# Value products held back until two groups of transposes are done, in a two-layer attention kernel

## The chip, the core and the metric

The kernel runs on one core of one Trainium2 chip. The metric is the device time of one execution in microseconds (us); lower is better. In the text PE is the matrix engine (TensorE), DVE is VectorE, ACT is ScalarE, POOL is GpSimd.

## What is computed

The reference is a trunk of two layers on 2048 rows of width 1024, in float32. Each layer projects the normalised input, runs attention, gates the result, projects it out and adds it to the input. Cut to the attention:

```
# layer 0: 8 heads of forgetting attention ("fox") and 4 of differential attention ("diff")
p  = softmax(where(causal, q @ k.T * scale + F[q] - F[k], -inf));  out = p @ v           # fox
p  = softmax(s1) - lam * softmax(s2);                              out = p @ v           # diff
# layer 1: 16 heads of dilated windows, branches merged by their softmax sums
sc = where(window_of_256_keys, q_blocks @ k_band.T * scale, -inf)
m, l = max(sc), sum(exp(sc - m));  o = (exp(sc - m) / l) @ v_band
```

## The kernel before

The projections, the attention of layer 0, its output projection, the projections of layer 1, its attention and its output projection follow one another. The change touches the two attentions, which share one scheduler (`run`) and one transposing helper (`flip`).

**Slots.** Layer 0's attention works on eight pairs `p`: `p` below 4 is a pair of fox heads, the others are one diff head with its two softmax maps. A unit is one block of 128 queries (block `i` has `i + 1` key tiles of 128). Its key tiles are cut into groups: four tiles of two heads for fox, eight tiles of one map for diff. Layer 1's units (`dilated`) are two query tiles of one branch, with one or two groups of up to eight blocks. One group is one slot of `run`, and a group has a weight (its fourth entry): 1 for fox and dilated, 2 for a diff group of more than four key tiles.

**What a slot does.** `grp[0]` is `turn`: it calls `flip`, which transposes up to eight 128x128 blocks of probabilities on PE. Each block goes as two halves of 64 rows, into two PSUM tiles `t_ps` (tag `t`, three buffers in all); then ACT or DVE, by a counter, copies each of the two tiles into a half of one SBUF tile `pt`. `emit` then issues the pieces that are due, mostly scores for a unit some slots later (`LEAD` is 7, `DLEAD` is 4). A score piece is 6 or 12 matmuls into two PSUM tiles `s_ps` (tag `s`, three buffers), and DVE reduces both tiles into SBUF (lines L840, L843 and L845, or L1276). `flush` last issues the value products (`grp[1]`, `av`) of the slot before, from its `pt` into an `o_ps` tile (tag `o`, two buffers). [...]

**On PE** a slot is thus a run of transposes (L709, called T below), a score piece (L834 or L1268, S) and the value products of the slot before (L923 or L1309, O). T and S use 64 rows of the array at a time (`64*128` in the profile's shapes), O uses 128 rows (`128*64` for fox and dilated, `128*128` for diff). A value product stands twice in the profile's counts and once in the program order.

**Order.** The engines run their queues in order. The order inside a queue is fixed when the program is built: a scheduler takes the instructions about as they are written, and moves some where it expects a wait. The finishing steps of a unit (`grp[2]`, row sums and the merge of branches) are queued by `flush` and run at the start of a later unit. In the diff part they use a tile `sq`.

Of the kernel before, what the change touches and what calls it, by code (L numbers as in the profile page):

```python
# [8 lines left out]
F32 = mybir.dt.float32  # L9
# [74 lines left out]
def trunk(ctx: ExitStack, tc: tile.TileContext, A, out):  # L84
# [6 lines left out]
    def dma(o, i):  # L91
        if o.dtype == F32R:
            o = o.bitcast(F32)
        if i.dtype == F32R:
            i = i.bitcast(F32)
        return queue[0].dma_start(o, i)  # L96
# [7 lines left out]
    def dap(t, off, ap):  # L104
        return bass.AP(tensor=t.tensor, offset=t.offset + off, ap=ap)

    def pool(es, name, bufs=1, space=None, side=None):
        kw = {"space": space} if space is not None else {}
        if side is not None:
            kw["side"] = side  # L110
        return es.enter_context(tc.tile_pool(name=name, bufs=bufs, reuse_waits="tile", **kw))
# [538 lines left out]
    def run(units, early):  # L650

        later, pend, slots, at, T = [], [], [], [], 0
        begins = []
        for n, (_, groups) in enumerate(units):
            begins.append(T)
            for grp in groups:  # L660
                slots.append((n, grp))
                at.append(T)
                T += grp[3]
        todo = [(begins[n] + when, f) for n, (pieces, _) in enumerate(units) for when, f in pieces]
        todo.sort(key=lambda x: x[0])

        def emit(until):
            while todo and todo[0][0] < until:
                todo.pop(0)[1]()

        def follow(n):
            for x in [x for x in later if x[0] <= n]:
                later.remove(x)
                x[1]()

        def flush():
            for n, grp in pend:
                grp[1]()
                later.extend((n + d, f) for d, f in grp[2])
            pend.clear()  # L680

        emit(0)
        for i, (n, grp) in enumerate(slots):
            if i == 0 or slots[i - 1][0] != n:
                follow(n)
            grp[0]()
            emit(at[i] + grp[3])
            flush()
            pend.append((n, grp))
        flush()  # L690
        for _ in early():
            n += 1
            follow(n)
        for _, f in sorted(later, key=lambda x: x[0]):
            f()
# [20 lines left out]
    def to_rows(ap, ps, x, n, rd, k, w):  # L716

        TE.transpose(ps[0:n, 0:128], x, ident)
        rh = ap.tile([128, 128], F32R, tag="rh", name="rh", bufs=1)
        rl = ap.tile([128, 128], F32R, tag="rl", name="rl", bufs=1)  # L720
        SC.copy(rh[0:n], ps[0:n, 0:128])
        V.tensor_tensor(rl[0:n], ps[0:n, 0:128], rh[0:n].bitcast(F32), OP.subtract)
        dma(dap(rd, 0, [[128, n], [1, 128]]), rh[0:n])
        dma(dap(rd, k * w, [[128, n], [1, 128]]), rl[0:n])
# [11 lines left out]
    def attention0():  # L736
# [5 lines left out]
        ap2 = pool(es, "at2")  # L742
# [199 lines left out]
        def finish(p, half):  # L942

            rd = row_d[2 * (p % 4) + half]

            def rows():
                lt = lts[p, half]
                x = x_bank("x_ps")
                if p < 4:
                    V.reciprocal(lt, lt)  # L950
                    to_rows(ap2, x, lt.rearrange("p h t -> p (h t)"), 16, rd, 2, 1024)
                else:

                    l1 = lt[:, 0, :]
                    V.scalar_tensor_tensor(l1, l1, 128.0 * EPS, l1, OP.mult, OP.mult)
                    to_rows(ap2, x, l1, 8, rd, 1, 1024)

            def chunk(n):
                c = HALVES[half][n]
                cs = slice(512 * c, 512 * c + 512)  # L960
                r = rw[n]
                x = x_bank("bc_ps")
                if p < 4:
                    dma(r[0:4], dap(rd, 512 * n, [[1024, 4], [1, 512]]))
                    og = gates[p]
                    TE.matmul(x, sels[0][0:64], r[0:64], start=True, stop=True)
                    V.tensor_tensor(og[:, cs], x, og[:, cs], OP.mult)
                else:
                    dma(r[0:2], dap(rd, 512 * n, [[1024, 2], [1, 512]]))
                    og = ogs[p]  # L970
                    sq = ap2.tile([128, 512], F32, tag="sq", name="sq", bufs=2)
                    SC.activation(sq, og[:, cs], AF.Square)
                    TE.matmul(x, ones, sq, start=True, stop=False)
                    TE.matmul(x, sels[1], r, start=False, stop=True)
                    SC.activation(sq, x, AF.Ln, scale=1.0 / 128)
                    SC.activation(sq, sq, AF.Exp, scale=-0.5)
                    (V if p == 7 else PO).tensor_tensor(sq, sq, gates[p][:, cs], OP.mult)
                    V.scalar_tensor_tensor(og[:, cs], og[:, cs], subl, sq, OP.mult, OP.mult)
                dma(og_d[0][c][p], og[:, cs])

            return [(1, rows), (LATE[p == 7][0], lambda: chunk(0)), (LATE[p == 7][1], lambda: chunk(1))]

        lts, Os, ogs, raws = {}, {}, {}, []
# [3 lines left out]
        def early():  # L987
# [10 lines left out]
            box.extend((wo, ps_p, (yield from first_rows(0, wo, ps_p, *ts, lambda e: split_raw(e) if e > 5 else None, 8))))  # L998

        run(units, early)  # L1000
        es.close()
        return box
# [1 line left out]

    WO_AT = [(0, 3), (0, 5), (0, 7), (1, 1), (1, 6), (1, 7)]
    LATE = ((3, 4), (2, 2))
    LEAD, PT_BUFS = 7, 3
    wo_es = ExitStack()
    wo_tiles = attention0()

# [135 lines left out]
    def dilated():  # L1146
# [252 lines left out]
        def early():  # L1399
# [6 lines left out]
            box.extend((wo, ps_p, (yield from first_rows(1, wo, ps_p, *ts, more_weights, 7))))  # L1406

        run([unit(p, c, br, half) for p in range(8) for c in range(4) for half in range(2) for br in range(2)], early)
        es.close()
        return box  # L1410
# [57 lines left out]
```

## Time and profile before

| | us |
|---|---|
| median of three runs | 3220.56 (3219.57 to 3225.43) |
| the profiled execution: its time | 3230.95 |
| the profiled execution: its span, first to last instruction | 3228.9 |
| PE busy in the span | 3080.9 (95%) |
| fox part, 798 to 1190 us | 392 |
| diff part, 1190 to 1562 us | 372 |
| dilated part, 2503 to 3013 us | 510 |

The profiled execution is 10.4 us longer than the median of the runs. Ends of matmuls are modelled, so distances between matmuls are read from their starts. "Busy" counts a matmul that is held up inside a run of matmuls as busy too; a wait of PE can therefore hide in a run that is longer than others of its kind.

### The profile page before, as it was taken

Reading aid. Unit: us, or ns where it says so; the run is one execution under the profiler, and the core shown is the slowest. Engines: PE = TensorE matmul, PEld = TensorE weight load, DVE = VectorE, ACT = ScalarE, POOL = GpSimd, SP = SyncE. Lnnn points to the kernel's source line nnn. Section 1 sums busy time; section 2 is a strip of 40 time slices with the busy share of each in tenths; the row PEclk is TensorE's granted clock in tenths of the full one; section 3 lists DMA queues with packets and bytes.
Section 4 is the critical chain, followed back from the end, with each engine's and each line's share of the span. In section 5 each row is a group of like instructions: output and inputs, shape, how many; then the busy total and the mean of one; then the engine's idle time right before and its main releaser. Section 6 shows DMA issues by size and latency. Waiting matters only on the chain. (4 is left out here: it accounts for less than half of the span.)

```text
span 3228.9 us, 60884 instructions
## 1 busy us (share of the span) xinstructions
PE 3080.9 (95%) x24252; PEld 2517.8 (78%) x24252; DVE 1567.0 (49%) x4176; ACT 1282.1 (40%) x2954; POOL 511.9 (16%) x495
## 2 busy tenths in 40 slices
PE   7999999999999999999999999999999888888898
PEld 6978889987777777777777998888888777767687
DVE  6443421001777788888554402311100777767643
ACT  5311111112766656556442321111111867766321
POOL 3200100002333200000032202220000022123321
PEclk9999999999999999999999999999999999987799
DMA  7255542216222221211352324674314655553252
GB/s 263 84 177 188 174 149 86 72 63 224 101 74 101 74 93 64 76 55 65 99 179 96 131 86 139 202 217 142 113 66 144 182 173 176 178 156 119 92 175 98
DMA packets 272309, 415.27 MB, mean 129 GB/s; under 512 B 28172, under 2 KB 155788, under 8 KB 267032
## 3 DMA queue, kind: packets, MB, share of 16 engines
q1 hardware_dynamic: 268712, 399.58, 38.6%
q0 software_dynamic: 3312, 11.80, 1.2%
q8 instruction: 190, 3.11, 0.4%
q14 instruction: 95, 0.78, 0.1%
HBM read 259.23 MB, written 152.05 MB: 127 GB/s over the span
## 5 line engine op out<-in xcount | busy, mean ns | idle before, releaser
L246 PE MATMUL pj<-hl,wh 128*128 128x512 f32 x1536 | 389.8, 396 | 0.0
L246 PE MATMUL pj<-hh,wh 128*128 128x512 f32 x1536 | 389.2, 395 | 0.0
L246 PE MATMUL pj<-hh,wl 128*128 128x512 f32 x1536 | 388.9, 395 | 0.0
L834 PE MATMUL s_ps<-K,Q 64*128 64x512 f32 (+2 forms) x1920 | 338.2, 395 | 19.0 <-DVE P L843 15.0
L709 PE MATMUL t_ps<-cc,P 64*128 64x64 f32 x5536 | 314.4, 236 | 33.5 <-DVE pt L713 20.4
L246 PEld LDWEIGHTS pj<-hl,wh 128*128 128x128 f32 x1536 | 289.4, 189 | 69.0 <-issue 0.5
L246 PEld LDWEIGHTS pj<-hh,wl 128*128 128x128 f32 x1536 | 288.6, 188 | 68.6 <-issue 0.5
L854 ACT ACTIVATE P<-P,m 128x1664 f32<-128x1664 f32 (+15 forms) x256 | 306.8, 1200 | 87.8 <-DVE m L849 87.6
L246 PEld LDWEIGHTS pj<-hh,wh 128*128 128x128 f32 x1536 | 288.1, 188 | 68.3 <-issue 1.0
L709 PEld LDWEIGHTS t_ps<-cc,P 64*128 64x128 f32 x5536 | 245.2, 143 | 114.3 <-issue 61.0
L923 PEld LDWEIGHTS o_ps<-pt,v 128*64 128x64 f32 (+1 forms) x3264 | 253.8, 158 | 87.2 <-issue 52.9
L923 PE MATMUL o_ps<-pt,v 128*64 128x128 f32 (+1 forms) x3264 | 317.1, 286 | 2.9 <-ACT pt L713 2.7
L1278 ACT ACTIVATE P<-P,st 128x256 f32<-128x256 f32 (+3 forms) x512 | 266.9, 524 | 92.0 <-DVE st L1276 90.6
L713 ACT COPY pt<-t_ps 128x512 f32<-128x512 f32 (+7 forms) x448 | 213.3, 495 | 176.2 <-PE t_ps L709 163.7
L231 DVE TENSOR_TENSOR wl<-w,wh 128x512 fp32r<-128x512 f32 (+1 forms) x128 | 84.9, 705 | 405.2 <-ACT wh L230 405.2
L713 DVE COPY pt<-t_ps 128x512 f32<-128x512 f32 (+5 forms) x384 | 229.9, 609 | 87.8 <-PE t_ps L709 69.0
L1276 DVE CUSTOM_DVE_ANT_0 P<-s_ps,band 128x256 f32<-128x256 f32 (+3 forms) x512 | 204.6, 448 | 111.4 <-PE s_ps L1268 108.3
L834 PEld LDWEIGHTS s_ps<-K,Q 64*128 64x128 f32 x1920 | 202.4, 192 | 60.6 <-DVE P L843 24.9
L1268 PE MATMUL s_ps<-K,Q 64*128 64x256 f32 (+2 forms) x1536 | 193.6, 339 | 12.9 <-DVE st L1276 11.5
L1309 PE MATMUL o_ps<-pt,v 128*64 128x128 f32 x2272 | 178.6, 298 | 9.4 <-DMA v<-v 3.5
L267 ACT ACTIVATE hi<-pj 128x512 fp32r<-128x512 f32 x80 | 47.8, 597 | 350.0 <-PE pj L246 329.8
L840 DVE CUSTOM_DVE_ANT_0 P<-s_ps,F 128x512 f32<-128x512 f32 (+1 forms) x192 | 121.4, 669 | 109.7 <-PE s_ps L834 108.9
(245 smaller groups left out, 4371.6 us busy)
## 6 DMA issues: line engine op xcount, KB each, us to landing
Q<-q SPq DMA_DIRECT2D x31, 1024.0 KB
ada<-ada_w SPq DMA_DIRECT2D x96, 256.0 KB
sg<-t2k SPq DMA_DIRECT2D x64, 256.0 KB
xt<-x SPq DMA_DIRECT2D x32, 512.0 KB
w<-w SPq DMA_DIRECT2D x64, 256.0 KB
q<-yb SPq DMA_DIRECT2D x64, 256.0 KB
x<-x SPq DMA_DIRECT2D x28, 512.0 KB
w<-w0b SPq DMA_DIRECT2D x56, 256.0 KB
```

The lines of the kernel that those rows point to most:

```text
L231: V.tensor_tensor(wl[:, 2 * q:2 * q + 2, :n], w[:, :, :n], wh[:, 2 * q:2 * q + 2, :n].bitcast(F32), OP.subtract)
L246: TE.matmul(ps, a[:, d, 128 * j:128 * j + 128], b[:, d, :], start=n == 0, stop=n == 23)
L709: TE.transpose(ps[k][:, n], b[rs], ident[rs, rs])
L713: last_flip[eng is SC] = f(pt[:, :len(blocks), 64 * k:64 * k + 64], ps[k][:, :len(blocks)])
L834: TE.matmul(ps[j][:, :n], queries[p, i // 4][hs, a, qs], keys[p][b][hs, c0:c0 + n], start=first, stop=a == 1)
L840: V.tensor_tensor_reduce(P[:, c0:c0 + n], ps[j][:, :n], forgets[p][j][:, c0:c0 + n], 1.0, 3.0e38, OP.add, OP.min, m)
L854: SC.activation(P, P, AF.Exp, bias=lows[j], scale=-1.0, accum_out=lt[:, j, col:col + 1])
L923: TE.matmul(o[:, cs], values[p][:, b, hs], pts[j, b], start=b == 0, stop=b == i)
L1268: TE.matmul(ps[hh][:, o:o + N], q[hs, qs], t["keys"](kk[hs]), start=k == 0, stop=k == 2)
L1276: V.tensor_tensor_reduce(P[:, hh, j, :n], ps[hh][:, o:o + n], m[:, m.shape[1] - n:], 1.0, 3.0e38, OP.add, OP.min, mn)
L1278: SC.activation(P[:, hh, j, :n], P[:, hh, j, :n], AF.Exp, bias=mn, scale=-1.0, accum_out=l)
L1309: TE.matmul(to, values[p, br][:, kc, hs], where[hh, j, o, kc], start=k == 0, stop=k == n - 1)
```

## The change

`run` calls `flush` only when the groups that are held back have a total weight above 1. Two fox or dilated groups are transposed one after the other, each followed by the score piece of its slot, and then, after the transposes and scores of the next slot, both groups' products go. A diff group of weight 2 is flushed as before; one of weight 1 waits and goes together with the group behind it. Three `pt` tiles are then filled before the first is read, so `pt` gets a fourth buffer in layer 0 (layer 1 has six). To make room in SBUF, `sq` has one buffer instead of two.

```diff
             grp[0]()
             emit(at[i] + grp[3])
-            flush()
+            if sum(x[1][3] for x in pend) > 1:
+                flush()
             pend.append((n, grp))
         flush()
...
-                    sq = ap2.tile([128, 512], F32, tag="sq", name="sq", bufs=2)
+                    sq = ap2.tile([128, 512], F32, tag="sq", name="sq", bufs=1)
...
-    LEAD, PT_BUFS = 7, 3
+    LEAD, PT_BUFS = 7, 4
```

The first place is on PE near the start of the fox part, at the end of one unit (tiles P_6269 and P_6272) and the one-tile unit behind it (P_6320 and P_6323). Line numbers of the changed kernel are 1 or 2 higher. Before:

```order
L834 MATMUL s_ps<-K,Q 128x256 x6
L923 MATMUL o_ps<-pt,v 64x128 x8
L709 MATMUL t_ps<-cc,P_6269 128x64 x2
L709 MATMUL t_ps<-cc,P_6272 128x64 x2
L834 MATMUL s_ps<-K,Q 128x512 x6
L923 MATMUL o_ps<-pt,v 64x128 x8
L709 MATMUL t_ps<-cc,P_6320 128x64 x2
L709 MATMUL t_ps<-cc,P_6323 128x64 x2
L834 MATMUL s_ps<-K,Q 128x512 x6
L923 MATMUL o_ps<-pt,v 64x128 x2
```

On the same queue at the same place, now:

```order
L836 MATMUL s_ps<-K,Q 128x256 x6
L925 MATMUL o_ps<-pt,v 64x128 x16
L711 MATMUL t_ps<-cc,P_6269 128x64 x2
L711 MATMUL t_ps<-cc,P_6272 128x64 x2
L836 MATMUL s_ps<-K,Q 128x512 x6
L711 MATMUL t_ps<-cc,P_6320 128x64
L711 MATMUL t_ps<-cc,P_6323 128x64
L836 MATMUL s_ps<-K,Q 128x512 x2
L711 MATMUL t_ps<-cc,P_6320 128x64
L711 MATMUL t_ps<-cc,P_6323 128x64
L836 MATMUL s_ps<-K,Q 128x512 x4
L925 MATMUL o_ps<-pt,v 64x128 x10
```

The eight products that stood between the two runs of transposes have moved behind the second score piece, where they join the next group's.

The second place is on PE in the dilated part, at the end of one head pair's units and the start of the next pair's. Before:

```order
L709 MATMUL t_ps<-cc,P 128x64 x16
L1268 MATMUL s_ps<-K,Q 128x256 x12
L1309 MATMUL o_ps<-pt,v 64x4x32 x8
L709 MATMUL t_ps<-cc,P 128x64 x16
L1268 MATMUL s_ps<-K,Q 128x256 x12
L709 MATMUL t_ps<-cc,P 128x64 x16
L1268 MATMUL s_ps<-K,Q 128x256 x12
L1309 MATMUL o_ps<-pt,v 64x128 x16
L709 MATMUL t_ps<-cc,P 128x64 x8
L1268 MATMUL s_ps<-K,Q 128x256 x12
L1309 MATMUL o_ps<-pt,v 64x4x32 x8
```

On the same queue, now:

```order
L711 MATMUL t_ps<-cc,P 128x64 x16
L1270 MATMUL s_ps<-K,Q 128x256 x12
L1311 MATMUL o_ps<-pt,v 64x4x32 x8
L711 MATMUL t_ps<-cc,P 128x64 x16
L1270 MATMUL s_ps<-K,Q 128x256 x12
L711 MATMUL t_ps<-cc,P 128x64 x8
L1270 MATMUL s_ps<-K,Q 128x256 x6
L1311 MATMUL o_ps<-pt,v 64x128
L1270 MATMUL s_ps<-K,Q 128x256 x6
L1311 MATMUL o_ps<-pt,v 64x128 x15
L1311 MATMUL o_ps<-pt,v 64x4x32 x8
```

Before, one pair of slots had no products between its transposes here, since a unit of two groups has products only behind its second; now the next pair of slots has none either, and three slots' products stand in two places instead of three (one product alone is set into the middle of a score piece).

Over the whole program order, runs of value products with no transpose or score between them go from 161 to 93 in the fox part, from 123 to 94 in the diff part and from 148 to 118 in the dilated part. Places where a score piece is followed directly by transposes go from 10 to 82, from 14 to 50 and from 21 to 69.

## Rows read from the trace of the kernel before

**Rows 1.** The page: busy us of each engine (share of the span), instructions.

```profile
PE 3080.9 (95%) x24252; PEld 2517.8 (78%) x24252; DVE 1567.0 (49%) x4176; ACT 1282.1 (40%) x2954; POOL 511.9 (16%) x495
```

**Rows 2.** Stretches fox, diff, dilated: length, busy us PE, PEld, DVE, ACT, POOL; clock.

```profile
798.00:1190.00 392.00, 380.49 (x5500) 289.79 (x5500) 290.81 (x943) 262.12 (x500) 110.29 (x120) 0.99 0.29 93
1190.00:1562.00 372.00, 354.68 (x2856) 263.69 (x2854) 309.60 (x939) 223.73 (x421) 15.37 (x12) 0.95 0.21 67
2503.00:3013.00 510.00, 448.96 (x5987) 365.81 (x5987) 384.59 (x1360) 359.62 (x1207) 110.10 (x91) 0.88 0.52 161
```

**Rows 3.** Waits of PE in the fox part, the longest: us, times, longest one.

```profile
PE t_ps L709 <- ACT pt L713: 6.2, 12, 1.3
```

**Rows 4.** Timeline of PE, one full fox slot: start us, length, instructions.

```profile
1007.25 0.71 PE L709 MATMUL t_ps<-cc,P 64*128 64x64 f32 x16
1007.77 0.94 PE L834 MATMUL s_ps<-K,Q 64*128 64x512 f32 x6
1008.64 1.09 PE L923 MATMUL o_ps<-pt,v 128*64 128x128 f32 x16
...
1009.66 0.71 PE L709 MATMUL t_ps<-cc,P 64*128 64x64 f32 x16
```

**Rows 5.** Timeline of PE in the dilated part, around a slot without products.

```profile
2554.77 0.97 PE L1268 MATMUL s_ps<-K,Q 64*128 64x256 f32 x12
...
2555.66 1.09 PE L1309 MATMUL o_ps<-pt,v 128*64 128x128 f32 x16
...
2556.69 0.71 PE L709 MATMUL t_ps<-cc,P 64*128 64x64 f32 x16
...
2557.21 0.96 PE L1268 MATMUL s_ps<-K,Q 64*128 64x256 f32 x12
...
2558.01 0.82 PE L709 MATMUL t_ps<-cc,P 64*128 64x64 f32 x15
...
2558.64 0.36 PE L1268 MATMUL s_ps<-K,Q 64*128 64x256 f32 x1
...
2559.50 0.95 PE L1268 MATMUL s_ps<-K,Q 64*128 64x256 f32 x11 [0.50 <-DVE st L1276]
...
2560.38 1.97 PE L1309 MATMUL o_ps<-pt,v 128*64 128x128 f32 x32
```

**Rows 6.** The same stretch on DVE: copies of transposes, then the third reduction.

```profile
2557.43 1.29 DVE L713 COPY pt<-t_ps 128x512 f32<-128x512 f32 x2 [0.47 <-PE t_ps L709]
...
2559.06 0.29 DVE L1276 CUSTOM_DVE_ANT_0 P<-s_ps,band 128x128 f32<-128x128 f32 x1
```

**Rows 7.** Timeline of a fox stretch: scores, ACT's copies, the first reduction, an exponential.

```profile
1005.78 0.94 PE L834 MATMUL s_ps<-K,Q 64*128 64x512 f32 x6
1006.06 1.07 ACT L713 COPY pt<-t_ps 128x512 f32<-128x512 f32 x2 [0.57 <-PE t_ps L709]
...
1006.76 0.69 DVE L840 CUSTOM_DVE_ANT_0 P<-s_ps,F 128x512 f32<-128x512 f32 x1 [1.06 <-PE s_ps L834]
...
1010.27 2.01 ACT L854 ACTIVATE P<-P,m 128x2048 f32<-128x2048 f32 x1 [1.61 <-DVE m L849]
```

**Rows 8.** Timeline of PE, fox: two runs of transposes, four products between them.

```profile
898.85 0.72 PE L709 MATMUL t_ps<-cc,P 64*128 64x64 f32 x16
...
899.87 1.13 PE L709 MATMUL t_ps<-cc,P 64*128 64x64 f32 x16
```

**Rows 9.** Timeline of PE, dilated: first and last row of another such slot.

```profile
2802.97 0.71 PE L709 MATMUL t_ps<-cc,P 64*128 64x64 f32 x16
...
2806.23 1.97 PE L1309 MATMUL o_ps<-pt,v 128*64 128x128 f32 x32
```

**Rows 10.** Timeline of PE, diff: two score pieces in a row.

```profile
1211.16 2.39 PE L834 MATMUL s_ps<-K,Q 64*128 64x256 f32 x12
```

**Rows 11.** A stretch at the end of the dilated part, columns as in rows 2.

```profile
2960.00:3040.00 80.00, 68.03 (x583) 52.78 (x584) 58.98 (x142) 38.59 (x104) 34.00 (x28) 0.72 0.22 69
```

**Rows 12.** Instructions on tile sq, POOL's multiply: ns min/median/max, first and last start.

```profile
L977 POOL TENSOR_TENSOR sq<-sq,sg x12: 1269/1280/1293, 1233.2 to 1502.7; 128x512 f32<-128x512 f32 x12
```

## The prediction

> **What bounds the kernel now.** I read the page's busy times first, then the stretches of the two attentions, then PE's timeline, and last DVE's and ACT's around it. PE is busy 95% of the span and no other engine passes half [rows 1], so time is gained where PE gets through its queue sooner and lost where it stands. The stretches differ [rows 2]. In the fox part PE is busy 380.5 of 392 us, and its longest entry of waits is 6.2 us [rows 3]; a full slot is T 0.52, S 0.87 and O 1.02 us from start to start, 2.41 us with no visible wait [rows 4]. In the diff part DVE is busy 309.6 of 372 us, and a run of twelve scores lasts 2.39 us where six of the wider kind take 0.94 [rows 4, 10]: PE already waits there inside the runs of scores. In the dilated part PE is idle 61 of 510 us. So fox is bound by PE alone, diff by PE and DVE together, dilated by the waits among three engines.
>
> **What is removed.** 127 runs of value products join a neighbour (68 in fox, 29 in diff, 30 in dilated, by the counts of the program order). What a run costs for being one is read off at its two ends. In front: twelve scores of 256 take 0.89 us to the next start when products follow and 0.80 when transposes follow [rows 5], so 0.09 us. Behind and at its first products: 16 products last 1.09 us and 32 last 1.97, that is 0.055 each or 0.88 for 16, yet from the first of 16 to the next transpose 1.03 us pass [rows 5], so 0.15 us. Together 0.24 us a run, and 127 x 0.24 = 30.5 us saved. The products themselves, the transposes, the scores, the copies and all DMAs stay as many as they were.
>
> [...]
>
> **What is added: two transposes and two score pieces with nothing between.** A score piece now meets transposes directly at 72 more places in fox, 36 in diff and 48 in dilated. Before, about 1 us of products stood there, and under it DVE and ACT emptied PSUM. There are three `s_ps` and three `t_ps` tiles, and a piece or a flip takes two: the second of a pair needs one tile of the first back. PE's queue is in order, so behind a transpose or a score that waits stand the rest of its run, the next scores and both groups of products, and for these DVE, ACT and the next units wait in turn.
>
> *Fox.* Scores start at 1005.78; DVE begins to reduce their first tile 0.98 us later and needs 0.69 [rows 7], so it is done at 1.67. With T and S alone between, the next scores start at 0.78 (0.87 less the 0.09 that go) + 0.52 = 1.30. The wait is 0.37 us if the tile is free at that instant. From the end of a reduction to PE going on, 0.15 us pass (the third one ends at 2559.35, the scores go on at 2559.50 [rows 5, 6]), which makes 0.52. I take 0.45, between the two. The transposes can wait as well: with four products between them, a second run of 16 takes 1.13 us instead of 0.72 [rows 8], and an exponential of 2.01 us on ACT [rows 7] would hold its copies longer. But what they lose shortens the scores' wait, so I don't add it. Narrower scores are reduced sooner; then the copies (two take 1.07 us, begun 0.28 us after the scores [rows 7]) set the wait, of about the same size. 72 x 0.45 = 32.4 us (26.6 to 37.4), less 68 x 0.24 = 16.3: **+16 us**, +10 to +21.
>
> *Dilated.* This order exists before the change, since a unit of two groups has a slot without products: T at 2556.69, S, T, S, and products at 2560.38, 3.69 us; the same four without a wait are 0.52 + 0.80 + 0.52 + 0.89 = 2.73 [rows 5]. So 0.96 us are waited, first for DVE's copies, then until the third reduction frees the first `s_ps` [rows 5, 6]. Another such place takes 3.26 us, a wait of 0.53 [rows 9]. The mean is 0.75. Of it I count half, since PE already idles 61 us in this part and a wait at one place takes the place of one behind it; the bounds are nothing and the full 0.96. 48 x 0.37 = 18 us, less 30 x 0.24 = 7.2: **+11 us**, -7 to +39.
>
> *Diff.* DVE sets the pace for much of it, so both the saving (29 x 0.24 = 7.0 us) and the new waits (36 x 0.45 = 16 us at most) may vanish in waits that are there. No row shows the new order here; I take 0.2 us a place, between nothing and fox's price: 7.2 - 7.0 = **0**, -7 to +9.
>
> **The smaller edits.** The fourth `pt` keeps a copy from waiting for the held products: three are filled before the first is read, the fourth takes the next flip. No cost. With one `sq`, the second chunk's square waits behind the first chunk's chain, POOL's 1.28 us above all [rows 12], eight times: up to 10 us on ACT. ACT is busy 224 of 372 us in diff [rows 2], and the scheduler has set the square behind that chain, so I take nothing; if that cover were gone, 10 us.
>
> **Sum.** 16 + 0 + 11 = +27 us on the profiled execution's 3230.95, so 3258; on the runs' median of 3220.56, **3248 us**. [...]
>
> [...]
>
> **Rivals.**
>
> *Faster: the tiles come back in time.* If DVE and ACT, with nothing in their queues, free them before PE needs them, only the saving stays: 3221 - 30.5 = 3190. For it: fox's own waits are small [rows 3], and the longer runs of products let DVE and ACT catch up before the next pair. Against it: rows 5, 7, 8 and 9 show the wait with idle engines too. It decides below 30.5 / 156 places = 0.20 us a place. Chance 0.22.
>
> *No difference.* Fox waits at its lower bound, and dilated and diff absorb theirs: +10 - 3 - 7 = 0, 3221. For it: 61 idle us in dilated [rows 2]. Chance 0.12.
>
> *Slower still, by the clock.* [...] Chance 0.06.
>
> That the change doesn't do what it says is no case: the program order shows it.
>
> **How the numbers follow.** The forecast has 0.60; its own range is 3217 (-4: +10 - 7 - 7) to 3290 (+69: +21 + 9 + 39). A measurement of this kernel can tell about 0.2%, 6.4 us, from no change. Slower: the forecast and the clock, 0.66. Same: 0.12. Faster: 0.22. The range for 8 in 10 goes from 3194, which keeps in most of the rival that is faster, to 3285, which leaves out the clock's and the far end of the forecast.
>
> **What would show it.** Right: fox some 16 us longer, with runs of 32 products of 1.97 us, T behind S longer than 0.72 us, and S split by waits for DVE's reductions; the dilated part longer by about 11, its waits now for `st` and `pt`. Wrong: second transposes of 0.72 us with scores 0.52 behind them, and fox down to 376 us. Then the tiles were free. If fox is longer and dilated shorter, the half that I let be absorbed was too little. [...]

## The result and the profile after

The changed kernel takes 3262.40 us (median of 4 runs, 3259.48 to 3269.90) against 3220.07 (median of 4, 3219.32 to 3225.43) for the kernel before: a ratio of 1.013, 95% interval 1.0105 to 1.0154, so 42 us slower (34 to 50). The profiled execution after took 3259.78 us, its span 3257.7. It lies 3 us below its median, while that of before lay 11 above its own, so profile against profile the change costs only 29 us. What follows goes by medians where times are compared, and by the traces for where they are spent.

The page of after (busy us, share, instructions), to be read against [rows 1]:

```profile
PE 3093.3 (95%) x24252; PEld 2551.0 (78%) x24252; DVE 1560.6 (48%) x4176; ACT 1289.3 (40%) x2954; POOL 512.3 (16%) x495
```

As many instructions as before. Here are the stretches that answer to [rows 2], same columns, moved by what the parts ahead of them had grown:

```profile
798.00:1213.00 415.00, 393.61 (x5490) 310.22 (x5489) 288.75 (x944) 264.87 (x500) 110.19 (x120) 0.98 0.27 88
1213.00:1591.00 378.00, 349.67 (x2867) 265.81 (x2868) 309.43 (x946) 226.45 (x423) 15.44 (x12) 0.96 0.21 67
2531.00:3043.00 512.00, 453.59 (x5937) 376.32 (x5939) 381.24 (x1356) 360.67 (x1202) 109.85 (x90) 0.91 0.52 160
```

Fox needs 415 us for what took 392, with the clock near full in both (0.98 and 0.99); diff 378 for 372; dilated 512 for 510, at a clock of 0.91 instead of 0.88. These stretches are not quite the parts themselves: before as after, fox's holds the first 20 us of diff (diff's first transpose starts at 1169.93 us before). The table at the end of the experiments has the parts by their own first instructions. In the fox stretch PE is idle 21 us instead of 12, so the larger part of the 23 us is not idle time at all. The groups of PE's lines in it show where it is (line, shapes, count, busy us, mean ns of one, idle us before them and their releasers). Before:

```profile
L923 PE MATMUL o_ps<-pt,v 128*64 128x128 f32 (+1 forms) x2230 | 163.3, 281 | 0.9 <-ACT pt L713 0.7
L834 PE MATMUL s_ps<-K,Q 64*128 64x512 f32 (+2 forms) x1011 | 156.5, 388 | 2.1 <-DVE P L843 1.6
L709 PE MATMUL t_ps<-cc,P 64*128 64x64 f32 x2236 | 118.9, 231 | 6.5 <-ACT pt L713 6.2 <-DVE pt L713 0.2
```

After:

```profile
L836 PE MATMUL s_ps<-K,Q 64*128 64x512 f32 (+2 forms) x1010 | 177.6, 394 | 3.3 <-DVE P L845 1.3 <-DVE m L842 1.3
L925 PE MATMUL o_ps<-pt,v 128*64 128x128 f32 (+1 forms) x2221 | 152.5, 282 | 0.0
L711 PE MATMUL t_ps<-cc,P 64*128 64x64 f32 x2236 | 129.0, 230 | 17.6 <-ACT pt L715 15.1 <-DVE pt L715 1.2
```

Value products O fell by 10.8 us. Scores S rose by 21.1 us busy and 1.2 idle, transposes T by 10.1 busy and 11.1 idle. (Busy times of the groups overlap, so these don't add up to the 23 us.) One score matmul lasts as long as before, 394 ns for 388, and there are as many; yet together they cover 177.6 us instead of 156.5. Before, 1011 x 0.388 = 392 us of matmuls lay in 156.5 us, 2.5 at a time; after, 398 lie in 177.6, 2.2 at a time. The two heads of a piece use 64 rows of the array each (`64*128` above) and mostly run side by side, as the 2.5 at a time and the count below show. Where only one head has a free PSUM tile, its first matmul starts alone, and the other head's wait is booked as busy. One such place, the second score piece of a pair:

```profile
869.60 0.95 PE L836 MATMUL s_ps<-K,Q 64*128 64x512 f32 x6
870.39 0.66 PE L711 MATMUL t_ps<-cc,P 64*128 64x64 f32 x16
870.85 1.45 PE L836 MATMUL s_ps<-K,Q 64*128 64x512 f32 x6
```

And DVE's first reduction of the first piece:

```profile
870.58 0.69 DVE L842 CUSTOM_DVE_ANT_0 P<-s_ps,F 128x512 f32<-128x512 f32 x1 [0.23 <-PE s_ps L836]
```

Of the second piece's six matmuls one starts at 870.85 and the next two at 871.34, 0.07 us after that reduction has ended. The piece takes 1.45 us instead of 0.95, of which only 0.01 is shown as idle. Counted over fox (ends of matmuls are modelled), just one score matmul is under way for 47 us, against 19 before.

A place where the transposes wait, timeline of PE in after:

```profile
1023.75 0.59 PE L711 MATMUL t_ps<-cc,P 64*128 64x64 f32 x12
1024.15 0.93 PE L836 MATMUL s_ps<-K,Q 64*128 64x512 f32 x6
1024.92 0.40 PE L711 MATMUL t_ps<-cc,P 64*128 64x64 f32 x4
1026.83 0.40 PE L711 MATMUL t_ps<-cc,P 64*128 64x64 f32 x5 [1.51 <-ACT pt L715]
1027.04 0.41 PE L836 MATMUL s_ps<-K,Q 64*128 64x384 f32 x1
1027.06 0.35 PE L711 MATMUL t_ps<-cc,P 64*128 64x64 f32 x3
1027.22 0.76 PE L836 MATMUL s_ps<-K,Q 64*128 64x384 f32 x5
1027.92 1.75 PE L925 MATMUL o_ps<-pt,v 128*64 128x128 f32 x28
```

And ACT beneath it:

```profile
1021.62 2.01 ACT L856 ACTIVATE P<-P,m 128x2048 f32<-128x2048 f32 x1 [0.23 <-DVE m L851]
...
1023.63 1.99 ACT L856 ACTIVATE P<-P,m 128x2048 f32<-128x2048 f32 x1
...
1025.61 0.71 ACT L856 ACTIVATE P<-P,m 128x512 f32<-128x512 f32 x1
...
1026.32 0.83 ACT L715 COPY pt<-t_ps 128x384 f32<-128x384 f32 x2
```

The second flip's transposes begin and stop after four: their other `t_ps` is still full, because its copy stands in ACT's queue behind three exponentials. PE goes on 0.51 us after the copies begin. The products now come in runs of 28 or 32, as the change meant.

### The profile page after: what moved, and what is told of

It is laid out like the page before. It is cut to its first block, busy times and chain, and to the rows that moved or that the text cites. A ratio compares the mean times of both kernels' runs of the same rounds, so it can differ in the third digit from the quotient of the medians.

```text
span 3257.7 us, 60888 instructions
## 1 busy us (share of the span) xinstructions
PE 3093.3 (95%) x24252; PEld 2551.0 (78%) x24252; DVE 1560.6 (48%) x4176; ACT 1289.3 (40%) x2954; POOL 512.3 (16%) x495
## 5 line engine op out<-in xcount | busy, mean ns | idle before, releaser
L836 PE MATMUL s_ps<-K,Q 64*128 64x512 f32 (+2 forms) x1920 | 360.7, 401 | 26.5 <-DVE P L845 19.9
L711 PE MATMUL t_ps<-cc,P 64*128 64x64 f32 x5536 | 335.0, 233 | 41.7 <-ACT pt L715 19.9
L711 PEld LDWEIGHTS t_ps<-cc,P 64*128 64x128 f32 x5536 | 264.0, 141 | 124.4 <-ACT pt L715 45.3
L925 PE MATMUL o_ps<-pt,v 128*64 128x128 f32 (+1 forms) x3264 | 297.9, 285 | 3.1 <-ACT pt L715 2.9
L836 PEld LDWEIGHTS s_ps<-K,Q 64*128 64x128 f32 x1920 | 214.3, 193 | 82.8 <-DVE P L845 33.6
L1270 PE MATMUL s_ps<-K,Q 64*128 64x256 f32 (+2 forms) x1536 | 208.2, 337 | 17.0 <-DVE st L1278 14.8
L1270 PEld LDWEIGHTS s_ps<-K,Q 64*128 64x128 f32 x1536 | 152.0, 199 | 37.6 <-DVE st L1278 26.3
```

Source lines behind the costliest of these rows:

```text
L711: TE.transpose(ps[k][:, n], b[rs], ident[rs, rs])
L836: TE.matmul(ps[j][:, :n], queries[p, i // 4][hs, a, qs], keys[p][b][hs, c0:c0 + n], start=first, stop=a == 1)
L925: TE.matmul(o[:, cs], values[p][:, b, hs], pts[j, b], start=b == 0, stop=b == i)
L1270: TE.matmul(ps[hh][:, o:o + N], q[hs, qs], t["keys"](kk[hs]), start=k == 0, stop=k == 2)
```

## Experiments

Two traces name two suspects, and the smaller edits a third. **Theory A:** each new place where T follows S waits for PSUM tiles, in fox above all. **Theory B:** the loss comes from elsewhere (the smaller edits, dilated, the clock). Within A, **theory S** (the prediction's): the score tiles that DVE reduces; **theory T:** the `t_ps` tiles whose copies stand behind exponentials. For all but one of the kernels below `run` takes a function that says how much weight may be held back (`n` counts layer 0's 128 units; the first 64 are fox):

```diff
-    def run(units, early):
+    def run(units, early, limit):
...
-            if sum(x[1][3] for x in pend) > 1:
+            if sum(x[1][3] for x in pend) > limit(n):
```

With 0 products are flushed in every slot, as before; with 1 in pairs, as after. Each ratio is to the kernel before, timed in turns with the others; its medians there are 3225.09, 3224.39 and 3224.82 us. Ranges in brackets are 95% intervals.

**Pairs in fox alone**

```diff
-        run(units, early)
+        run(units, early, lambda n: 1 if n < 64 else 0)
```

(dilated: `lambda n: 0`.)

> Pairs of groups only in the fox half of the first attention; the diff half and the dilated attention flush in every slot as before; the fourth `pt` and the single `sq` stay. Theory A (each place where scores and transposes meet without products waits for a PSUM tile, and fox is where this costs more than the saved runs give back): about 3243 us, 20 to 25 over the kernel before, as much as the fox part grew in the trace of the changed kernel (371.5 to 394.4 us). Theory B (the time is lost elsewhere: in the smaller edits, in the dilated attention, or through the clock): under 3230.

Measured: 3255.23 us, ratio 1.009 (1.007 to 1.0109): 29 us (23 to 35), more than either number. Fox itself grew by 23 us in the trace, as theory A said; the rest lies elsewhere, and the smaller edits, which this kernel keeps, are measured below.

**Pairs in the first attention** (fox and diff: `lambda n: 1` there, 0 in dilated)

> Pairs in both halves of the first attention, none in the dilated attention; the smaller edits stay. Theory A: 3248 to 3256 us, that is 28 to 36 over the kernel before: fox's 23 and diff's 6 from the two traces, and at most a few more. Theory B (dilated carries much of the loss): under 3240.

Measured: 3263.95 us, the median of five executions (a sixth took 11776 us and is left out), ratio 1.0121 (1.0093 to 1.0149), 39 us (30 to 48). Theory A in sign; its range, 28 to 36, lies a little lower.

**Pairs in dilated alone** (0 in the first attention, 1 in dilated; two `sq`, three `pt`)

> Pairs only in the dilated attention; first attention, `pt` and `sq` as before the change. Theory A (the waits of a new place are mostly absorbed by idle time that the part has anyway): 3217 to 3226 us, no difference that this measurement can tell from none. Theory B (each of 48 places costs the whole 0.75 us that such places show): 3220 + 36 - 7 = 3249. The number of the prediction was +11: 3231.

Measured: 3231.15 us, ratio 1.0016 (1.0001 to 1.0031): 5 us, between nothing and 10. The whole 0.75 us a place is excluded, and so, narrowly, is the prediction's +11.

**The smaller edits alone** (0 everywhere)

> Products flushed in every slot as before; only the fourth `pt` and the single `sq`. Theory A: 3220 us, no difference. Theory B (the single `sq` holds ACT behind POOL's chain in the second half of the first attention): up to 3230.

Measured: 3237.28 us, ratio 1.0031 (1.0019 to 1.0043): 10 us (6 to 14). Here theory B was right, and the number was the one that the prediction gave for a lost cover. With it the other kernels fit: fox costs 0.90 - 0.31 = 0.59%, 19 us.

**One of the two smaller edits**

```diff
-    LEAD, PT_BUFS = 7, 4
+    LEAD, PT_BUFS = 7, 3
```

(one `sq`, products flushed in every slot.)

> Of the whole change only the single `sq`; three `pt`, products flushed in every slot. If `sq` is what the smaller edits cost (3237 against 3224 of the kernel before in the last runs): 3234 to 3237. If it is the fourth `pt`: 3224, no difference.

Measured: 3234.95 us, ratio 1.0031 (1.002 to 1.0042), as much as both edits together. So `sq` is what costs, and the fourth `pt` nothing, to within 5 us. Before, the two chunks of a diff head go through ACT one behind the other; their first steps on the summed squares:

```profile
1545.62 0.60 ACT L975 ACTIVATE sq<-bc_ps 128x512 f32<-128x512 f32 x1 [1.81 <-PE bc_ps L974]
...
1546.86 0.59 ACT L975 ACTIVATE sq<-bc_ps 128x512 f32<-128x512 f32 x1
...
1550.80 1.47 ACT L854 ACTIVATE P<-P,m 128x1408 f32<-128x1408 f32 x1 [2.69 <-DVE m L849]
```

With one `sq`, at the same place:

```profile
1545.19 0.60 ACT L977 ACTIVATE sq<-bc_ps 128x512 f32<-128x512 f32 x1 [1.90 <-PE bc_ps L976]
...
1547.99 0.63 ACT L974 ACTIVATE sq<-og 128x512 f32<-128x512 f32 x1 [0.80 <-DVE og L980]
1550.13 0.60 ACT L977 ACTIVATE sq<-bc_ps 128x512 f32<-128x512 f32 x1 [1.51 <-PE bc_ps L976]
...
1555.82 1.47 ACT L856 ACTIVATE P<-P,m 128x1408 f32<-128x1408 f32 x1 [4.43 <-DVE m L851]
```

And DVE there:

```profile
1546.48 0.69 DVE L979 TENSOR_TENSOR sq<-sq,sg 128x512 f32<-128x512 f32 x1 [3.19 <-ACT sq L978]
...
1550.96 0.69 DVE L845 TENSOR_SCALAR_CACHE_REDUCE P<-s_ps 128x512 f32<-128x512 f32 x1 [3.00 <-PE s_ps L836]
```

The second square waits until DVE has finished the first chunk's `og`, and the chunk's two matmuls on PE (L975, L976) follow it, with the next scores behind them. DVE stands idle for 3.0 us, for these scores, and ACT's next exponentials begin 10.6 us after the first chunk's step instead of 5.2. PE's waits for reduced score tiles (L836 on L845, 1169 to 1589 us) rise from 13.5 to 17.4 us. ACT itself waited only 0.8 us for `sq` in diff: here the price is paid on PE and DVE, not on the engine that the prediction looked at. This is one place of eight. The whole diff part of this trace is 4 us longer than before, that of the smaller edits 9, so how the 10 us are spread over the places is not shown.

**Pairs in diff alone** (0 in fox and dilated, 1 in diff; smaller edits kept)

> Pairs only in the diff half of the first attention; the smaller edits stay, so it is read against 3237 us. By the prediction the 36 new places and the 29 saved runs cancel: 3237. By the difference of the kernels with pairs in the first attention and in fox alone, +10: 3247. If DVE's pace hides the waits and the saving stays: 3230.

Measured: 3245.84 us, ratio 1.0059 (1.0044 to 1.0074), 0.28% above the smaller edits alone: 9 us (3 to 15). The second number held.

**The pairs without the smaller edits**

```diff
-                    sq = ap2.tile([128, 512], F32, tag="sq", name="sq", bufs=1)
+                    sq = ap2.tile([128, 512], F32, tag="sq", name="sq", bufs=2)
...
-    LEAD, PT_BUFS = 7, 4
+    LEAD, PT_BUFS = 7, 3
```

> Of the whole change only the pairs, in all parts; two `sq` and three `pt` as before. If `sq` costs 10 us and a fourth `pt` is worth nothing to the pairs: 3250 to 3254, 10 under the changed kernel and some 28 over the kernel before. If the pairs need the fourth `pt`: 3262 or more, since a copy would then wait for the held products.

Measured: 3251.11 us, ratio 1.0084 (1.0066 to 1.0101), 27 us over the kernel before. The pairs don't need a fourth `pt`. Fox and dilated alone make 19 + 5, so with two `sq` the pairs in diff cost about 3 us, give or take 10.

**A PSUM bank more for the scores, without and with pairs.** A layer 0 `o_ps` now collects four consecutive units, two from each of the two query chunks that are worked on in turn, and is emptied in two pieces (not shown); that frees one PSUM tile of 128x512 f32, called a bank here.

```diff
-                ps = [aps.tile([128, 512], F32, tag="s", name="s_ps", bufs=3) for _ in range(2)]
+                ps = [aps.tile([128, 512], F32, tag="s", name="s_ps", bufs=4) for _ in range(2)]
...
-                if i % 4 == 0 and g == 0:
-                    Os[p, c] = aps.tile([128, 512], F32, tag="o", name="o_ps", bufs=2)
-                O = Os[p, c]
-                cs = slice(128 * (i % 4), 128 * (i % 4) + 128)
+                if k % 4 == 0 and g == 0:
+                    Os[p, half] = aps.tile([128, 512], F32, tag="o", name="o_ps", bufs=1)
+                O = Os[p, half]
+                cs = slice(128 * (k % 4), 128 * (k % 4) + 128)
...
```

> The first attention gathers the products of four units in one PSUM tile (`o_ps` once instead of twice, emptied in two halves), and the freed bank makes a fourth `s_ps`. Products are flushed in every slot; the smaller edits stay. This is the base for the kernel with pairs, and is read against the kernel with the smaller edits alone (3237 us). Both theories: 3230 to 3250; the scores hardly wait in fox (1.6 us before), and the single `o_ps` may cost a few us.

> The same layout with the fourth `s_ps`, and pairs in both halves of the first attention. Theory S (the step of the prediction: the second score piece of a pair waits for a score tile that DVE still reduces): the waits go and the saving of 97 runs stays, so 10 to 25 us under the same layout without pairs. Theory T (the second transposes wait for a `t_ps` whose copy stands behind an exponential on ACT): a score tile more changes nothing of that, so 20 to 30 us over the same layout without pairs, as in the three-tile layout (3264 against 3237).

Measured: 3211.29 us without pairs, ratio 0.996 (0.9946 to 0.9975), and 3223.89 with, 0.9995 (0.9979 to 1.0012). Both keep the single `sq`, so the layout is to be read against the smaller edits alone (1.0031): it gains 0.71%, 23 us (17 to 29), which neither theory had. Pairs cost 0.35% in it, 11 us (4 to 18), instead of 0.90%, 29 us (19 to 39), with three score tiles. Theory S had said a gain of 10 to 25 us, theory T a loss of 20 to 30; neither holds.

**The same bank for the transposes** (`t_ps` four times, `s_ps` three)

> The layout with one `o_ps`, and the freed bank as a fourth `t_ps`; products flushed in every slot, the smaller edits stay. The base for the kernel with pairs. Both theories: 3225 to 3245, perhaps a little under the layout with a fourth `s_ps`, since the transposes of fox wait 6.2 us for copies even without pairs.

> The fourth `t_ps`, and pairs in both halves of the first attention. Theory S: the waits for score tiles stay, 20 to 30 us over the same layout without pairs. Theory T: two flips of a pair find their four tiles empty and the saving of 97 runs stays, 5 to 25 us under the same layout without pairs. A result between (-5 to +20) would say that both tiles are waited for, one behind the other.

Measured: 3230.89 us without pairs, 1.0026 (1.0009 to 1.0043), and 3241.89 with, 1.0059 (1.0038 to 1.008). Without pairs this bank gains nothing that can be told from the smaller edits alone; it was expected perhaps a little under the layout for the scores and is 20 us above it. Pairs cost 0.33%, 11 us (2 to 19). Either bank takes away about 18 of the 29 us (give or take 12), neither all: the result between, for both tiles. In the traces the pairs lengthen fox by 20 us with three of each, by 8 with four `s_ps` and by 6 with four `t_ps`. A fourth of both was not run. The groups of PE's lines, 800 to 1192 us in the fox part, with pairs and four `s_ps`:

```profile
L836 PE MATMUL s_ps<-K,Q 64*128 64x512 f32 (+2 forms) x993 | 153.3, 389 | 0.8 <-DVE P L845 0.6 <-DVE m L842 0.2
...
L711 PE MATMUL t_ps<-cc,P 64*128 64x64 f32 x2233 | 127.6, 231 | 24.5 <-ACT pt L715 20.9 <-DVE pt L715 1.4 <-DVE P L881 1.0
```

With pairs and four `t_ps`:

```profile
L836 PE MATMUL s_ps<-K,Q 64*128 64x512 f32 (+2 forms) x993 | 183.5, 397 | 10.6 <-DVE m L842 3.7 <-DVE m L847 2.1 <-DVE P L845 1.8
...
L711 PE MATMUL t_ps<-cc,P 64*128 64x64 f32 x2232 | 109.4, 227 | 0.2 <-ACT pt L715 0.2
```

(The windows hold 17 score matmuls fewer than those above.) With four `s_ps` the scores' extra 21 us are gone (153.3, as before) and T waits longer, 24.5 us for 17.6. With four `t_ps` the transposes' wait is gone (0.2) and S waits longer, 10.6 us for 3.3. The time with just one score matmul under way says the same: 47 us with pairs and three of each, 23 with four `s_ps`, 58 with four `t_ps`. The place shown above, with four `t_ps`:

```profile
1019.01 0.59 PE L711 MATMUL t_ps<-cc,P 64*128 64x64 f32 x12
1019.41 0.94 PE L836 MATMUL s_ps<-K,Q 64*128 64x512 f32 x6
1020.18 0.53 PE L711 MATMUL t_ps<-cc,P 64*128 64x64 f32 x12
1020.52 0.41 PE L836 MATMUL s_ps<-K,Q 64*128 64x384 f32 x1
1021.14 0.79 PE L836 MATMUL s_ps<-K,Q 64*128 64x384 f32 x5 [0.20 <-DVE m L842]
1021.86 1.75 PE L925 MATMUL o_ps<-pt,v 128*64 128x128 f32 x28
```

From the first transpose to the products 2.85 us pass instead of 4.17. The transposes run through, and the next thing to stop is a score piece, for a tile that DVE reduces.

**The faster version:** four `s_ps`, no pairs, two `sq`, three `pt`.

> The layout with one `o_ps` and four `s_ps`, products flushed in every slot, two `sq` and three `pt` as before: that is, the kernel before with another use of one PSUM bank. With the single `sq` this layout took 3211 us, 0.4% under the kernel before. Theory S for the diff half (its waits for score tiles, 13.5 us in the trace of before, go) and 10 us for `sq` give 3200 to 3204, 20 to 24 under the kernel before; if `sq` costs nothing in this layout, 3211.

Measured: 3206.03 us, ratio 0.9939 (0.9923 to 0.9955): 20 us under the kernel before (15 to 25), close to the first number. It gains in diff, where the time with just one score matmul under way falls from 65 to 28 us. There, twelve scores behind fourteen transposes took 4.06 us before, at the first of these rows, and take 2.79 at the second:

```profile
1299.99 4.06 PE L834 MATMUL s_ps<-K,Q 64*128 64x512 f32 x12
```

```profile
1289.74 2.79 PE L836 MATMUL s_ps<-K,Q 64*128 64x512 f32 x12
```

Lengths of the parts in the profiled executions, by starts on PE: fox from its first transpose to diff's (798.35 and 1192.76 in after), diff from there to the first `y_ps` matmul (1606.45), dilated from its first score (2531.00) to the next `y_ps` (3060.41).

| kernel | fox | diff | dilated |
|---|---|---|---|
| before | 371.5 | 407.4 | 527.8 |
| after | 394.4 | 413.7 | 529.4 |
| pairs in fox / in diff / in both | 394.6 / 374.6 / 391.7 | 413.6 / 420.5 / 421.9 | 531.5 / 522.3 / 519.3 |
| pairs in dilated alone | 371.1 | 405.2 | 532.2 |
| smaller edits / `sq` alone | 371.4 / 372.5 | 416.1 / 411.4 | 529.7 / 524.2 |
| pairs without smaller edits | 390.4 | 399.8 | 527.9 |
| four `s_ps`, single / pairs | 369.0 / 376.7 | 391.9 / 394.6 | 522.8 / 528.9 |
| four `t_ps`, single / pairs | 371.5 / 377.4 | 412.2 / 420.1 | 529.2 / 525.8 |
| the faster version | 367.7 | 388.5 | 516.3 |

All but before, pairs in dilated alone, pairs without smaller edits and the faster version have the single `sq`. Fox repeats within some 4 us among kernels with the same fox. Dilated does not: with the same code it takes 516 to 532 us, so one trace can't show a change of 5 us there. Diff lies between the two: with one `sq`, three `s_ps` and three `t_ps` it takes 411 to 416 us in three kernels without pairs and 414 to 422 in three with.

## Why the prediction came out as it did

The forecast (slower, 3248, within 3194 to 3285) was right in sign, and its main mechanism, the wait for PSUM tiles in fox, is shown; 14 us were missing, and the terms that make them up were off in both directions, three of them too small and one too large, which hid 6 us of the miss. By differences of timed kernels: fox +19, smaller edits +10, diff +9, dilated +5, together 43 for the 42 measured; predicted were +16, 0, 0 and +11.

- **Saved per run, 0.24 us.** The part behind a run (0.15) fits: O's busy time in fox falls by 10.8 us for 68 runs, 0.16 each. The part in front (0.09) is drowned in the scores' waits and not shown apart.
- **Fox, +16: 19 by the runs (12 to 26), 23 in the trace.** If 16.3 us are saved, 72 places cost 35 to 39 us, 0.49 to 0.54 each, for 0.45 taken and 0.37 to 0.52 allowed. The wait of the scores is as predicted: at the place shown DVE begins 0.98 us after the scores and the piece loses 0.50 us, though the first head goes on alone and only the second waits. The step "what they lose shortens the scores' wait, so I don't add it" holds only in part. With four `t_ps` the transposes' 17 us of idle time go and the scores wait longer, by 7 us idle and more in busy time, but 14 of fox's 20 us go too (391.7 to 377.4). So the copies behind ACT's exponentials had a price of their own, which the sum left out.
- **Dilated, +11: 5 (0 to 10).** A half was too much to count: (5 + 7.2) / 48 = 0.25 us a place, a third of 0.75. The scores of PE there (2500 to 3062 us), before and after:

```profile
L1268 PE MATMUL s_ps<-K,Q 64*128 64x256 f32 (+2 forms) x1536 | 193.6, 339 | 12.9 <-DVE st L1276 11.5 <-ACT t2k L311 0.7 <-ACT rt L1337 0.3
L1270 PE MATMUL s_ps<-K,Q 64*128 64x256 f32 (+2 forms) x1536 | 208.2, 337 | 17.0 <-DVE st L1278 14.8 <-ACT t2k L311 0.7
```

  The same matmuls, no longer each, cover 15 us more and wait 4 us more before them. All three kernels with pairs in dilated show it (207 to 209 us busy), none of the eleven without (190 to 197). So the waits for DVE came, and once more most of them are booked as busy. Why only 5 us are left is not settled. PE waits less before value products there (4.9 to 5.8 us with pairs, 7.5 to 10.0 without), its waits for POOL overlap (16.6 to 23.9 us in the three with pairs, 21.6 and 19.0 in two without, before and pairs in the first attention), and the granted clock is higher (last section).
- **Diff, 0: +9 (3 to 15) with one `sq`, about 3 with two.** The upper bound was +9. The two numbers are too uncertain to tell apart, and diff's length in the traces moves by several us without any edit to it. The trace without the smaller edits even has it 8 us shorter than before. Whether the term comes from pairs and the single `sq` together is not shown.
- **The smaller edits, 0: +10 (6 to 14).** The step that failed: "the scheduler has set the square behind that chain, so I take nothing". The order inside the queue was as read, but the first chunk's chain is long (2.80 us at the place shown, from ACT's step on it to the second square), and behind the second chunk's matmuls stand PE's scores, for which DVE waits 3.0 us there. The sum was taken from ACT's idle time alone.
- **Rivals.** "Faster" needed under 0.20 us a place; fox has 0.5. "No difference" needed fox at +10 and the other two parts to give 10 back; fox took 19, and neither gave any back. For "slower still, by the clock" no run shows a loss: in dilated the clock did not fall but rose, 0.91 for 0.88.

## What to carry over

Where an engine's queue is in order and its tiles are few, as PE's three `s_ps` and three `t_ps` here, the work that stands between two uses of a tile is the time in which it is emptied, and a place without it cost 0.49 to 0.54 us in fox: count tiles against uses in a row before joining runs, on every side that empties them. A wait can hide in busy time, as in fox, where the scores' busy time rose by 21.1 us and the idle time before them by 1.2, so compare count times mean length with busy time, and look for pairs that no longer run side by side. A buffer given up "to make room" is a change of its own and deserves its own run; here it cost half as much as the main edit in fox, and a PSUM bank moved to the scores gained 20 us where holding products back lost 27.

## What was not expected of the hardware

In dilated, pairs go with a higher granted clock, 0.91 after for 0.88 before. These are means: in the clock records of the two traces it is 1 or 0.5 at any time, and 0.5 for 118 of the 510 us from 2503 before and for 86 of the 510 us from 2531 after. Stretches of 510 us from the start of that part, with pairs in it (pairs in dilated alone, then all pairs without the smaller edits):

```profile
2501.00:3011.00 510.00, 449.19 (x5913) 372.70 (x5914) 376.34 (x1344) 358.06 (x1197) 109.89 (x90) 0.92 0.51 159
```

```profile
2518.00:3028.00 510.00, 451.41 (x5943) 374.24 (x5943) 380.62 (x1353) 360.45 (x1202) 109.86 (x90) 0.92 0.52 160
```

Without pairs in it (pairs in fox alone):

```profile
2531.00:3041.00 510.00, 457.23 (x5941) 371.99 (x5943) 380.91 (x1350) 356.94 (x1199) 109.87 (x90) 0.86 0.52 161
```

All three kernels with pairs in dilated were granted 0.91 or 0.92 there, all eleven without 0.86 to 0.89, though PE was busy as much (449 to 452 us against 446 to 457). One transpose there lasts 234 to 235 ns in the three and 241 to 245 in the eleven. The higher clock may be part of why dilated lost so little. As an estimate from the two records, 32 us fewer at 0.5 are worth up to 16 us if all of it were PE's. No run separates it from the waits, and why the clock rose is open.
